# Sums of the merge, the projections and the FFN on VectorE, and each branch for both token halves

## The chip, the core and the metric

The program runs on one core of a Trainium2 chip. A core has a matrix engine (TensorE; the profile calls it PE, and its weight loads PEld), a vector engine (VectorE, DVE), a scalar engine (ScalarE, ACT), a general engine (GpSimd, POOL) and a sync engine (SyncE, SP) which here issues every DMA. Each engine takes its instructions from a queue of its own, in order; semaphores tie the queues together. The metric is the device time of one execution in microseconds. Three runs of the kernel took 1720.38, 1725.53 and 1726.62 us; the median is 1725.53.

## The reference

One layer of a decoder over 1024 tokens of width 1024, all in float32:

```
merged = gate_a * (y_a @ w_branch_a) + gate_b * (y_b @ w_branch_b)
x = x + gate1 * (merged @ w_out)
h2 = rms_norm(x, norm2_gain) * (1 + scale2) + shift2
ffn = (silu(h2 @ ffn_w1) * (h2 @ ffn_w3)) @ ffn_w2
x = x + gate2 * ffn
```

`y_a` (1024x512) is the output of an RWKV-7 recurrence and `y_b` (1024x512) that of sliding-window attention; both, and the gates, come from an input projection of the normed x. `gate1`, `shift2`, `scale2` and `gate2` are sections of a vector made from the conditioning input. The FFN's inner width is 2816.

## The kernel before

Every matmul of float32 operands is done as three (`mm3`, L140 to L144): each operand is split into a rounded part (`hi`, ScalarE) and the rest (`lo`, VectorE), and PE adds lo x hi, hi x lo and hi x hi. A matmul here is mostly 128x128 against 128x512. So each operand needs one ScalarE cast and one VectorE subtraction of a 128x512 tile (or 128x1024, `load_split`, L114) before PE can use it.

The program has five stages. The mixer (0 to about 828 us) runs the recurrence and the attention and leaves `y_a`, `y_b` and the gates in DRAM, transposed: features on partitions, tokens along the row, in two halves of 512 tokens. Then come the branches, the output projection with the second norm, the FFN's first two matrices and the FFN's out projection.

In `branches` (L1001) one token half h is done at a time. For each of eight column blocks j it loads and splits 128 columns of both branch weights (one 128x1024 tile), loads the two gate tiles, and for each branch i runs 4 k x 3 matmuls into a PSUM bank; VectorE multiplies the bank by the gate (L1019), and `sub` (L1054), which is GpSimd's `tensor_tensor` unless another engine is named, adds the two (L1022). That is 192 matmuls for a half. `after0` and `after1` (L1168, L1188) put the loads of the output projection's weights (`wo`, multiplied by `gate1b`, L1166) and its sums beside the branches.

The output projection is a Strassen-like form with seven products of 512x512x512 in place of eight (`token_product`, L1065), 4 jj x 4 t x 3 = 48 matmuls each. Its operands are sums of the quadrants: S1o to S4o from the merged activations, T1o and the `wo_t2` to `wo_t4` from the weights, each a 128x512 `sub`. The order on PE is: branches of half 0, two products (which need half 0 only, into the banks `ya` and `xa`), branches of half 1 (into `xa`, `banks`, L1015), the five other products. `norm2(0)` (L1109) runs beside the last two products: it scales rows, transposes blocks on PE (L1132) and splits them; `norm2(1)` follows and makes also the B operands of the FFN, with two GpSimd subtractions in each of four steps (L1149, L1153).

The FFN works on 11 pairs of column blocks (jp), 7 products x 24 matmuls each (`hidden_first`, `hidden_rest`, L1268, L1278). For each jp there are eight sums of weights (s1, s2, s3, s4 for two i) and four sums of the results (`fs`, L1327 to L1334) on GpSimd; the sums that read PSUM are on VectorE already. The out projection has seven products of 11 jj (132 matmuls each) with weights `w2t` summed on GpSimd, and `finish` (L1379) has two GpSimd instructions for each of 16 less 4 output tiles.

The code of these stages is put in order by a scheduler that knows the dependencies; the place of an instruction in its engine's queue is fixed when the program is built. Names in the profile are those of the tiles: `gt`, `mg`, `wo`, `s1o`, `wpart` (a split weight or operand), `fs`, `s` (an FFN weight sum), `pgf` and `pgo` (PSUM banks), `ptr` (a transpose).

Of the kernel before, what the change touches and what calls it, by code (L numbers as in the profile page):

```python
# [19 lines left out]
P = 128  # L20
# [46 lines left out]
def block_kernel(ctx: ExitStack, tc: tile.TileContext, a: dict, out: bass.AP):  # L67
# [99 lines left out]
    def load_y(h, stage):  # L167
        ys = []
        for src, nm in ((ya_d, "ya"), (yb_d, "yb")):
            for p in range(NP):  # L170
                full = stage()
                nc.sync.dma_start(out=full, in_=src[h, p])
                ys.append(spl(full, f"{nm}{h}_{p}"))
        return ys
# [3 lines left out]
    with ExitStack() as mx:  # L178
# [716 lines left out]
        for h in range(NH):  # L895
# [33 lines left out]
            if h == NH - 1:  # L929
                wkx.close()  # L930
                act2 = ctx.enter_context(tc.tile_pool(name="act2", bufs=NB, side="right"))
                stages = iter(("ada_a", "ada_w") * 4)
                ys0 = load_y(0, lambda: mw.tile([P, HALF], F32, tag=next(stages), name="yst",
                                                bufs=1))
# [6 lines left out]
            for j in range(16):  # L941
                ps = proj_block(hT, 20 + j)
                gt = mw.tile([P, HALF + 1], F32, tag="tm", name="gt", bufs=3)

                nc.scalar.activation(out=gt[:, 0:HALF], in_=ps, func=AF.Tanh, scale=0.5,
                                     bias=hbg[:, j:j + 1])
                nc.sync.dma_start(out=gates_d[h, j], in_=gt[:, 0:HALF])


    with ExitStack() as fx:  # L950
# [50 lines left out]
        def branches(h, ys, banks=None, after=None):  # L1001
            mg = []
            for j in range(KT):
                cols = slice(j * P, (j + 1) * P)
                wh, wl = load_split(
                    lambda v: [(v[:, 0:4, :], wa_d[:, cols].rearrange("(k p) n -> p k n", p=P)),
                               (v[0:64, 4:8, :], wb_v[0, :, :, cols]),
                               (v[64:128, 4:8, :], wb_v[1, :, :, cols])], KT, P)
                gts = []
                for i in range(2):  # L1010
                    gt = st_tile("gt2")
                    nc.sync.dma_start(out=gt, in_=gates_d[h, 8 * i + j])
                    gts.append(gt)
                for i in range(2):
                    ps = banks[(2 * j + i) % 4] if banks else bank()  # L1015
                    for k in range(4 * i, 4 * i + 4):
                        mm3(ps, wh[:, k, :], wl[:, k, :], ys[k][0], ys[k][1], k % 4 == 0,
                            k % 4 == 3)
                    nc.vector.scalar_tensor_tensor(out=gts[i], in0=gts[i], scalar=1.0, in1=ps,  # L1019
                                                   op0=ALU.add, op1=ALU.mult)  # L1020
                mg.append(a_tile("mg"))
                sub(mg[j], gts[0], gts[1], ALU.add)  # L1022
                if after:
                    after(j, mg)
            return mg
# [83 lines left out]
        def norm2(h):  # L1109
# [35 lines left out]
            for k in range(4):  # L1145
# [3 lines left out]
                nc.gpsimd.tensor_tensor(out=t3, in0=b22, in1=b12, op=ALU.subtract)  # L1149
# [3 lines left out]
                nc.gpsimd.tensor_tensor(out=b12, in0=b22, in1=b12, op=ALU.subtract)  # L1153
# [4 lines left out]
        for i in range(3):  # L1158
            ada_loads(i, lambda: a_tile("acc2"))
        WO = {}  # L1160

        def wo_load(e, n, jj):
            WO[e, n, jj] = w = a_tile("wo")
# [4 lines left out]
        def after0(j, mg):  # L1168
            if j == 1:
                ada_section(0, gate1b)  # L1170
            if j in (2, 3, 4, 5):
                wo_load(0, 0, j - 2)
                wo_load(1, 0, j - 2)

        mg0 = branches(0, ys0, None, after0)
        ys1 = load_y(1, lambda: st_tile("yst"))
# [3 lines left out]
        token_product(xa, 4, lambda jj: mg0[2 * jj + 1], lambda jj: WO[1, 0, jj], True)  # L1180
        for t in range(4):
            sub(p1[t], p1[t], x_load(t, 0), ALU.add)
            x1[t][0] = sub(p1[t], xa[t], p1[t], ALU.add, nc.vector)
        ada_section(1, sh2)
        ada_section(2, sc2)
        S1o, S2o, S3o, S4o, T1o = ([None] * 4 for _ in range(5))

        def after1(j, mg):  # L1188
            jj = j // 2
            if j % 2 == 0:  # L1190
                wo_load(0, 1, jj)
                wo_load(1, 1, jj)
                T1o[jj] = sub(a_tile("t1o"), WO[0, 1, jj], WO[0, 0, jj])
                return
            a11, a12, a21, a22 = mg0[j - 1], mg0[j], mg[j - 1], mg[j]
            S1o[jj] = sub(a_tile("s1o"), a21, a22, ALU.add)
            S3o[jj] = sub(a21, a11, a21)
            S2o[jj] = sub(a_tile("s2o"), S1o[jj], a11)
            S4o[jj] = sub(a_tile("s4o"), a12, S2o[jj])
# [5 lines left out]
        def wo_t2(jj):  # L1205
            return sub(T1o[jj], WO[1, 1, jj], T1o[jj])

        def wo_t3(jj):
            return sub(WO[0, 1, jj], WO[1, 1, jj], WO[0, 1, jj])

        def wo_t4(jj):
            return sub(WO[1, 0, jj], WO[1, 0, jj], T1o[jj])

        token_product(ya, 4, lambda jj: S2o[jj], wo_t2, False)
        u1 = copies(ya, "u1")
        token_product(xa, 4, lambda jj: S4o[jj], lambda jj: WO[1, 1, jj], False)
        for t in range(4):
            sub(u1[t], u1[t], x_load(t, 1), ALU.add)
            x1[t][1] = sub(u1[t], xa[t], u1[t], ALU.add, nc.vector)
        norm2(0)  # L1220
        token_product(ya, 4, lambda jj: S3o[jj], wo_t3, False)
        for t in range(4):
            sub(p5[t], p5[t], x_load(4 + t, 1), ALU.add)
            x1[4 + t][1] = sub(p5[t], ya[t], p5[t], ALU.add, nc.vector)
            x1[4 + t][0] = x_load(4 + t, 0, temp)
        token_product(ya, 4, lambda jj: mg1[2 * jj + 1], wo_t4, False)
        for t in range(4):
            sub(x1[4 + t][0], ya[t], x1[4 + t][0], ALU.add, nc.vector)
# [49 lines left out]
        def hidden_rest(jp, ws, u2, f11):  # L1278
# [19 lines left out]
            for i in range(2):  # L1298
                sub(u2[i], ps[i], u2[i], ALU.add, nc.vector)
# [3 lines left out]
            for i in range(2):  # L1303
                u3[i] = temp("u3")
                sub(u3[i], ps[i], u2[i], ALU.add, nc.vector)
            ps = dense(lambda i: ws[i][3], "T4")
            for i in range(2):
                c[i] = temp("c21")
                sub(c[i], u3[i], ps[i], ALU.subtract, nc.vector)
# [4 lines left out]
            for i in range(2):  # L1314
                sub(u3[i], ps[i], u3[i], ALU.add, nc.vector)
# [3 lines left out]
            for i in range(2):  # L1319
                sub(u2[i], ps[i], u2[i], ALU.add, nc.vector)  # L1320
# [136 lines left out]
```

## Time and profile before

| | |
|---|---|
| runs, median | 1725.53 us (1720.38 to 1726.62) |
| profiled execution, its own time | 1723.27 us |
| span of the profiled execution, first to last instruction | 1720.8 us |
| PE busy | 1592.9 us, 93% |
| DVE, ACT, POOL busy | 67%, 41%, 34% of the span |
| mean granted TensorE clock | 0.963 of full speed |

The profiled execution is the one from which every row below is taken; 2.5 us of its time lie outside the span. PE's busy time counts matmuls in flight, so a stretch in which PE is busy from end to end can still be one in which it is slow: the granted clock tells that. The engines' shares are means over five stages with different limits.

### The profile page before, as it was taken

Reading aid. Unit: us, or ns where it says so; the run is one execution under the profiler, and the core shown is the slowest. Engines: PE = TensorE matmul, PEld = TensorE weight load, DVE = VectorE, ACT = ScalarE, POOL = GpSimd, SP = SyncE. Lnnn points to the kernel's source line nnn. Section 1 sums busy time; section 2 is a strip of 40 time slices with the busy share of each in tenths; the row PEclk is TensorE's granted clock in tenths of the full one; section 3 lists DMA queues with packets and bytes.
Section 4 is the critical chain, followed back from the end, with each engine's and each line's share of the span. In section 5 each row is a group of like instructions: output and inputs, shape, how many; then the busy total and the mean of one; then the engine's idle time right before and its main releaser. Section 6 shows DMA issues by size and latency. Waiting matters only on the chain. (4 is left out here: it accounts for less than half of the span.)

```text
span 1720.8 us, 24983 instructions
## 1 busy us (share of the span) xinstructions
PE 1592.9 (93%) x8835; PEld 1218.1 (71%) x8835; DVE 1156.2 (67%) x2560; ACT 712.1 (41%) x1346; POOL 579.1 (34%) x504
## 2 busy tenths in 40 slices
PE   3989988999989999999988698899999999999998
PEld 2756766666656777667877576687777777786887
DVE  7689777775567767875364577765555555689566
ACT  5454435445643233446241257323323332343442
POOL 6232121122331000000247821563333334689022
PEclk9998999999997998999999798999999999999999
DMA  9344446345443224325765235343323322871641
GB/s 306 101 138 128 118 130 169 111 127 176 124 128 93 58 79 108 96 77 181 223 184 160 68 120 156 122 153 120 101 92 98 97 94 74 287 253 60 198 151 50
DMA packets 234081, 228.19 MB, mean 133 GB/s; under 512 B 38850, under 2 KB 171084, under 8 KB 233956
## 3 DMA queue, kind: packets, MB, share of 16 engines
q1 hardware_dynamic: 233956, 226.60, 43.2%
q8 instruction: 69, 1.13, 0.3%
q14 instruction: 56, 0.46, 0.1%
HBM read 175.92 MB, written 50.63 MB: 132 GB/s over the span
## 5 line engine op out<-in xcount | busy, mean ns | idle before, releaser
L142 PE MATMUL pg<-hhi,wlo 128*128 128x512 f32 x480 | 201.9, 423 | 8.6 <-DVE wlo L134 5.5
L143 PE MATMUL pg<-hlo,whi 128*128 128x512 f32 x480 | 202.1, 421 | 0.0
L144 PE MATMUL pg<-hhi,whi 128*128 128x512 f32 x480 | 201.3, 420 | 0.0
L142 PE MATMUL pgo<-wpart 128*128 128x512 f32 x420 | 167.8, 399 | 15.0 <-DVE wpart L1051 7.8
L134 DVE TENSOR_TENSOR wlo<-wraw,whi 128x1024 fp32r<-128x1024 f32 x88 | 111.8, 1274 | 94.5 <-ACT whi L133 90.1
L143 PE MATMUL pgo<-wpart 128*128 128x512 f32 x420 | 167.8, 399 | 4.2 <-DVE wpart L1051 4.2
L144 PE MATMUL pgo<-wpart 128*128 128x512 f32 x420 | 166.7, 397 | 0.0
L885 POOL TENSOR_TENSOR aacc<-aacc,adaw 128x512 f32<-128x512 f32 x64 | 86.6, 1353 | 234.9 <-ACT adaw L884 221.6
L1051 DVE TENSOR_TENSOR wpart<-s,wpart 128x512 fp32r<-128x512 f32 x88 | 84.5, 960 | 85.8 <-ACT wpart L1050 83.8
L133 ACT CAST whi<-wraw 128x1024 fp32r<-128x1024 f32 x88 | 91.6, 1047 | 113.5 <-PE pg L144 56.3
L1055 POOL TENSOR_TENSOR fs<-fs 128x512 f32<-128x512 f32 x44 | 59.5, 1364 | 188.2 <-DVE fs L1260 186.6
L142 PEld LDWEIGHTS pg<-hhi,wlo 128*128 128x128 f32 x480 | 94.0, 196 | 35.9 <-DVE wlo L134 5.7
L1051 DVE TENSOR_TENSOR wpart<-fo,wpart 128x512 fp32r<-128x512 f32 x77 | 86.2, 1120 | 46.6 <-ACT wpart L1050 46.6
L1050 ACT CAST wpart<-s 128x512 fp32r<-128x512 f32 x88 | 54.6, 622 | 150.5 <-PE pgf L144 91.2
L143 PEld LDWEIGHTS pg<-hlo,whi 128*128 128x128 f32 x480 | 93.8, 195 | 21.6 <-issue 3.0
L144 PEld LDWEIGHTS pg<-hhi,whi 128*128 128x128 f32 x480 | 94.0, 196 | 20.0 <-issue 1.1
L142 PEld LDWEIGHTS pgo<-wpart 128*128 128x128 f32 x420 | 80.8, 192 | 34.4 <-DVE wpart L1051 9.1
L1055 DVE TENSOR_TENSOR u<-pgf,u 128x512 f32<-128x512 f32 x88 | 60.5, 687 | 60.8 <-PE pgf L144 60.7
L1050 ACT CAST wpart<-fo 128x512 fp32r<-128x512 f32 x77 | 47.9, 622 | 122.6 <-PE pgo L144 106.3
L143 PEld LDWEIGHTS pgo<-wpart 128*128 128x128 f32 x420 | 80.7, 192 | 24.0 <-DVE wpart L1051 7.6
L144 PEld LDWEIGHTS pgo<-wpart 128*128 128x128 f32 x420 | 80.7, 192 | 16.6
L619 DVE SCALAR_TENSOR_TENSOR tmpi<-ai,inv,rt 128x60 f32<-128x60 f32 (+24 forms) x248 | 71.8, 290 | 16.8 <-DMA ai<-a_scr 12.7
(583 smaller groups left out, 4126.8 us busy)
## 6 DMA issues: line engine op xcount, KB each, us to landing
wraw<-in_w_in_dram SPq DMA_DIRECT2D x72, 512.0 KB
wraw<-in_ffn_w_dram SPq DMA_DIRECT2D x56, 512.0 KB
f_d<-fs SPq DMA_DIRECT2D x77, 256.0 KB
fo<-f_d SPq DMA_DIRECT2D x77, 256.0 KB
adaw<-in_ada_w_dram SPq DMA_DIRECT2D x64, 256.0 KB
w2t<-in_ffn_w_dram SPq DMA_DIRECT2D x44, 256.0 KB
adaw<-in_ada_w_dram SPq DMA_DIRECT2D x8, 1024.0 KB
gates_d<-gt SPq DMA_DIRECT2D x32, 256.0 KB
```

The costliest lines, as they stand in the source:

```text
L133: nc.scalar.copy(out=hi, in_=raw)
L134: nc.vector.tensor_tensor(out=lo, in0=raw, in1=hi.bitcast(F32), op=ALU.subtract)
L142: nc.tensor.matmul(ps, lhsT=ll, rhs=rh, start=first, stop=False, skip_group_check=more)
L143: nc.tensor.matmul(ps, lhsT=lh, rhs=rl, start=False, stop=False, skip_group_check=more)
L144: nc.tensor.matmul(ps, lhsT=lh, rhs=rh, start=False, stop=last, skip_group_check=more)
L619: nc.vector.scalar_tensor_tensor(out=tv, in0=ai[:, jj, j + 1:32].unsqueeze(1).broadcast_to([P, m, n]), scalar=inv2[:, j:j + 1], in1=rt[:, ...
L885: nc.gpsimd.tensor_tensor(out=acc, in0=acc, in1=wt, op=ALU.add)
L1050: nc.scalar.copy(out=hi, in_=src)
L1051: nc.vector.tensor_tensor(out=lo, in0=src, in1=hi.bitcast(F32), op=ALU.subtract)
L1055: (eng or nc.gpsimd).tensor_tensor(out=out, in0=x, in1=y, op=op)
```

## The change

1. `sub` runs on VectorE, and with it every elementwise sum and product from the merge on, those of `norm2` and `finish` too. GpSimd has no work after the mixer; its queue shrinks from 391 rows to 180.
2. `branches(h)` becomes `branch(i)`: branch 1 (attention) for both token halves, then branch 0 for both. A weight tile is loaded and split once in a branch, 128x512, and used by both halves. Branch 1's gate tile is loaded into the `mg` tile and multiplied in place; branch 0's result is added to it.
3. The `wo` tiles and T1o to T4o are made in branch 1 (`after_b`), S1o to S4o in branch 0 (`after_a`). Three `y` parts are loaded and split in the mixer's last part, where there were two; `ysa[1]` is loaded between the branches.
4. The seven products stand in a row behind the branches. The third to the fifth are now S2, S1, S4 (before: S1, S2, S4).

```diff
-        def branches(h, ys, banks=None, after=None):
-            mg = []
+        def branch(i, ys, after):
+
             for j in range(KT):
                 cols = slice(j * P, (j + 1) * P)
                 wh, wl = load_split(
-                    lambda v: [(v[:, 0:4, :], wa_d[:, cols].rearrange("(k p) n -> p k n", p=P)),
-                               (v[0:64, 4:8, :], wb_v[0, :, :, cols]),
-                               (v[64:128, 4:8, :], wb_v[1, :, :, cols])], KT, P)
...
+                    lambda v: [(v[0:64], wb_v[0, :, :, cols]), (v[64:128], wb_v[1, :, :, cols])]
+                    if i else [(v, wa_d[:, cols].rearrange("(k p) n -> p k n", p=P))], 4, P)
+                for h in range(NH):
+                    gt = a_tile("mg") if i else st_tile("gt2")
                     nc.sync.dma_start(out=gt, in_=gates_d[h, 8 * i + j])
...
+                    ps = bank()
+                    for k in range(4):
+                        mm3(ps, wh[:, k, :], wl[:, k, :], ys[h][k][0], ys[h][k][1], k == 0, k == 3)
+                    nc.vector.scalar_tensor_tensor(out=gt, in0=gt, scalar=1.0, in1=ps,
                                                    op0=ALU.add, op1=ALU.mult)
-                mg.append(a_tile("mg"))
-                sub(mg[j], gts[0], gts[1], ALU.add)
...
+                    if i:
+                        mg[h].append(gt)
+                    else:
+                        sub(mg[h][j], mg[h][j], gt, ALU.add)
+                after(j)
...
-        def sub(out, x, y, op=ALU.subtract, eng=None):
-            (eng or nc.gpsimd).tensor_tensor(out=out, in0=x, in1=y, op=op)
+        def sub(out, x, y, op=ALU.subtract):
+            nc.vector.tensor_tensor(out=out, in0=x, in1=y, op=op)
             return out
...
+        def after_b(j):
+            if j == 0:
+                ada_section(0, gate1b)
+            if 1 <= j < 5:
+                for jj in range(4):
+                    wo_load(*((0, 0), (1, 0), (0, 1), (1, 1))[j - 1], jj)
+            if 4 <= j:
+                jj = j - 4
+                b11, b21, b12, b22 = (WO[x + (jj,)] for x in ((0, 0), (1, 0), (0, 1), (1, 1)))
+                T3o[jj] = sub(a_tile("t3o"), b22, b12)
+                T1o[jj] = sub(b12, b12, b11)
+                T2o[jj] = sub(a_tile("t2o"), b22, b12)
+                T4o[jj] = sub(a_tile("t4o"), b21, T2o[jj])
...
+        def after_a(j):
             if j == 1:
...
+                ada_section(1, sh2)
+                ada_section(2, sc2)
+            if j % 2 == 0:
+                return
+            jj = j // 2
+            a11, a12, a21, a22 = mg[0][j - 1], mg[0][j], mg[1][j - 1], mg[1][j]
+            S1o[jj] = sub(a_tile("s1o"), a21, a22, ALU.add)
+            S2o[jj] = sub(a_tile("s2o"), S1o[jj], a11)
+            S4o[jj] = sub(a_tile("s4o"), a12, S2o[jj])
+            S3o[jj] = sub(a21, a11, a21)
+
+        mg = [[], []]
+        ysa = [ysa0, None]
+        branch(1, ysb, after_b)
+        ysa[1] = load_y(ya_d, 1, lambda: st_tile("yst"))
+        branch(0, ysa, after_a)
         xa, ya = four(1), four(0)
-        token_product(ya, 4, lambda jj: mg0[2 * jj], lambda jj: WO[0, 0, jj], True)
+        token_product(ya, 4, lambda jj: mg[0][2 * jj], lambda jj: WO[0, 0, jj], True)
         p1 = copies(ya, "p1")
...
-        mg1 = branches(1, ys1, xa, after1)
+        token_product(ya, 4, lambda jj: S2o[jj], lambda jj: T2o[jj], False)
+        u1 = copies(ya, "u1")
         token_product(xa, 4, lambda jj: S1o[jj], lambda jj: T1o[jj], True)
         p5 = copies(xa, "p5")
...
         token_product(xa, 4, lambda jj: S4o[jj], lambda jj: WO[1, 1, jj], False)
```

On PE the 192 matmuls of the first branch are now followed at once by those of the second, and the first output product stands behind 384 branch matmuls.

On DVE, at the end of one FFN step and the start of the next, before: `u` and `fs` are results of the step that ends, `s` the weight sums of the next, `wraw` loaded weights.

```order
L1055 TENSOR_TENSOR u_12428<-pgf,u_12428 128x512
L1051 TENSOR_TENSOR wpart<-wraw,wpart 128x512
L1260 TENSOR_TENSOR fs<-fs,u_12428 128x512
L1051 TENSOR_TENSOR wpart<-s_12736,wpart 128x512
L1051 TENSOR_TENSOR wpart<-s_12740,wpart 128x512
L1051 TENSOR_TENSOR wpart<-s_12776,wpart 128x512
L1260 TENSOR_TENSOR fs<-fs,pgf 128x512
L1051 TENSOR_TENSOR wpart<-s_12779,wpart 128x512
```

The sums that make `s`, and the four `fs` sums of L1327 to L1334, are not in this queue: GpSimd makes them. (`fs<-fs,u` is the product of L1260.)

The same place of a step after the change:

```order
L1054 TENSOR_TENSOR u_13842<-pgf,u_13842 128x512
L1050 TENSOR_TENSOR wpart<-wraw,wpart 128x512
L1258 TENSOR_TENSOR fs<-fs,u_13842 128x512
L1054 TENSOR_TENSOR fs<-fs 128x512 x4
L1054 TENSOR_TENSOR s_14149<-wraw 128x512
L1054 TENSOR_TENSOR s_14150<-s_14149,wraw 128x512
L1054 TENSOR_TENSOR s_14153<-wraw 128x512
L1054 TENSOR_TENSOR s_14154<-s_14153,wraw 128x512
L1050 TENSOR_TENSOR wpart<-s_14150,wpart 128x512
L1054 TENSOR_TENSOR s_14190<-wraw 128x512
L1050 TENSOR_TENSOR wpart<-s_14154,wpart 128x512
L1054 TENSOR_TENSOR s_14193<-wraw 128x512
```

The four result sums (one row, `x4`) and the first four weight sums now stand between the last result and the first split of the next step; the other four follow between the splits.

On SP, at the end of branch 1 and the start of branch 0, after the change: `wraw` are branch weights, `mg` and `gt` gate tiles, `yst` the blocks of `ysa[1]`.

```order
L127 DMA wraw<-in_w_branch_a_dram 128x4x128
L1166 DMA wo<-in_w_out_dram 128x512 x2
L1014 DMA mg<-gates_d 128x512
L1166 DMA wo<-in_w_out_dram 128x512 x3
L127 DMA wraw<-in_w_branch_a_dram 128x4x128
L1166 DMA wo<-in_w_out_dram 128x512
L1014 DMA mg<-gates_d 128x512 x2
L1166 DMA wo<-in_w_out_dram 128x512 x2
L127 DMA wraw<-in_w_branch_a_dram 128x4x128
L1166 DMA wo<-in_w_out_dram 128x512 x2
L171 DMA yst<-ya_d 128x512 x4
L1014 DMA gt_9808<-gates_d 128x512
```

Gate loads, `wo` loads, the weights of the next branch and the `y` blocks share the one queue, and a weight load stands there until a `wraw` buffer is free.

The queue in the second half's branches before:

```order
L1012 DMA gt_10073<-gates_d 128x512
L1012 DMA gt_10075<-gates_d 128x512
L1012 DMA gt_10121<-gates_d 128x512
L127 DMA wraw<-in_w_branch_a_dram 128x4x128
L127 DMA wraw<-in_w_branch_b_dram 64x4x128
L127 DMA wraw<-in_w_branch_a_dram 128x4x128
L127 DMA wraw<-in_w_branch_b_dram 64x4x128
L127 DMA wraw<-in_w_branch_a_dram 128x4x128 x2
L127 DMA wraw<-in_w_branch_b_dram 64x4x128 x6
```

Each column block had three weight loads (both branches) and two gate loads there, for one half; now a column block of a branch has one weight load (two in branch 1) for both halves.

## Rows read from the trace of the kernel before

**Rows 1.** The windows by stage: busy time (and count) of each engine, clock, DMA.

```profile
...
core 0: us, PE busy (x) PEld busy (x) DVE busy (x) ACT busy (x) POOL busy (x), PEclk, DMA share, GB/s
...
870.00:945.00 75.00, 66.74 (x283) 53.46 (x282) 41.81 (x49) 22.28 (x35) 42.40 (x28) 0.98 0.63 178
945.00:985.00 40.00, 24.76 (x73) 18.52 (x74) 19.38 (x18) 11.07 (x21) 38.19 (x28) 0.74 0.22 72
985.00:1050.00 65.00, 58.36 (x270) 47.18 (x270) 50.56 (x118) 36.24 (x77) 11.03 (x8) 0.92 0.45 143
1050.00:1110.00 60.00, 50.20 (x204) 38.12 (x203) 41.28 (x52) 31.63 (x54) 28.69 (x19) 0.91 0.43 131
...
1160.00:1480.00 320.00, 313.43 (x1361) 253.81 (x1360) 170.31 (x226) 98.94 (x164) 136.61 (x98) 1.00 0.32 105
1480.00:1600.00 120.00, 113.41 (x490) 90.91 (x489) 108.54 (x95) 50.10 (x91) 90.98 (x56) 1.00 0.59 200
...
```

**Rows 2.** PE's timeline: first branch matmul, first FFN matmul, end; start us first.

```profile
...
827.76 0.50 PE L142 MATMUL pgf<-ya_0h,wlo 128*128 128x512 f32 x1
...
1037.53 0.40 PE L142 MATMUL pgf<-g0h,wpart 128*128 128x512 f32 x1
...
1713.25 0.39 PE L142 MATMUL pgo<-wpart 128*128 128x512 f32 x1
...
1715.74 0.39 PE L144 MATMUL pgo<-wpart 128*128 128x512 f32 x1
```

**Rows 3.** What PE waits for, 870 to 1110 us: us in total, times, longest.

```profile
PE pgo L142 <- DVE gt L1019: 11.4, 3, 5.5
PE pgo L142 <- DVE wpart L1051: 7.8, 2, 5.2
PE pgf L142 <- ACT bt_3h L1101: 5.1, 1, 5.1
PE ptr L1132 <- DVE xr L1126: 3.8, 1, 3.8
PE pgf L142 <- ACT u L1274: 3.7, 2, 3.3
...
```

**Rows 4.** DVE's instructions by line and form, 1110 to 1720 us.

```profile
...
L1051 DVE TENSOR_TENSOR wpart<-fo,wpart 128x512 fp32r<-128x512 f32 x77 | 86.2, 1120 | 46.6 <-ACT wpart L1050 46.6
...
L1055 DVE TENSOR_TENSOR u<-pgf,u 128x512 f32<-128x512 f32 x85 | 58.4, 687 | 56.7 <-PE pgf L144 56.7
...
L1051 DVE TENSOR_TENSOR wpart<-t1o,wpart 128x512 fp32r<-128x512 f32 x11 | 7.5, 684 | 0.0
...
```

**Rows 5.** What SP's queue waits for, 827 to 1045 us.

```profile
...
SPq L1012 <- POOL mg L1055: 34.0, 7, 7.5
...
```

**Rows 6.** The timeline of all engines at one FFN step's end, start us first.

```profile
...
1338.99 0.69 DVE L1055 TENSOR_TENSOR u<-pgf,u 128x512 f32<-128x512 f32 x1 [1.33 <-PE pgf L144]
...
1341.06 5.26 POOL L1055 TENSOR_TENSOR fs<-fs 128x512 f32<-128x512 f32 x4 [22.38 <-DVE fs L1260]
...
1348.97 0.62 ACT L1050 CAST wpart<-s 128x512 fp32r<-128x512 f32 x1 [3.84 <-POOL s L1055]
...
1349.62 1.11 DVE L1051 TENSOR_TENSOR wpart<-s,wpart 128x512 fp32r<-128x512 f32 x1 [8.64 <-ACT wpart L1050]
...
1350.79 0.50 PE L142 MATMUL pgf<-bt_0h,wpart 128*128 128x512 f32 x1 [0.82 <-DVE wpart L1051]
...
```

**Rows 7.** What PE waits for, 1160 to 1480 us.

```profile
PE pgf L142 <- DVE wpart L1051: 6.6, 8, 0.8
```

**Rows 8.** What PE waits for, 1480 to 1720 us.

```profile
PE pgo L143 <- DVE wpart L1051: 4.2, 8, 1.7
PE pgf L142 <- DVE u L1055: 2.4, 1, 2.4
```

**Rows 9.** The windows view of 20 us of the out projection.

```profile
1540.00:1560.00 20.00, 20.00 (x90) 16.58 (x89) 20.00 (x13) 8.12 (x15) 20.00 (x12) 1.00 0.32 95
```

**Rows 10.** What POOL waits for, 1480 to 1720 us.

```profile
...
POOL w2t L1055 <- DMA w2t<-in_ffn_w_dram: 11.2, 2, 10.4
...
```

More of the change, by code (lines that the diff above doesn't have):

```diff
@@ L165, in spl, with load_y @@
         return hi, lo
-    def load_y(h, stage):
+    def load_y(src, h, stage):
         ys = []
[L169 to L173, printed above, removed]
+        for p in range(NP):
+            full = stage()
+            nc.sync.dma_start(out=full, in_=src[h, p])
+            ys.append(spl(full, f"y{h}_{p}"))
         return ys
@@ L931, in block_kernel, with stage @@
                 act2 = ctx.enter_context(tc.tile_pool(name="act2", bufs=NB, side="right"))
-                stages = iter(("ada_a", "ada_w") * 4)
-                ys0 = load_y(0, lambda: mw.tile([P, HALF], F32, tag=next(stages), name="yst",
-                                                bufs=1))
+                stages = iter(("ada_a", "ada_w") * 6)
+                def stage():
+                    return mw.tile([P, HALF], F32, tag=next(stages), name="yst", bufs=1)
+                ysb = [load_y(yb_d, 0, stage)]
+                ysa0 = load_y(ya_d, 0, stage)
             mixer_step(h, NP, hT)
@@ L947, in block_kernel @@
                 nc.sync.dma_start(out=gates_d[h, j], in_=gt[:, 0:HALF])
+        ysb.append(load_y(yb_d, 1, stage))
     with ExitStack() as fx:
@@ L1158, in block_kernel @@
         for i in range(3):
-            ada_loads(i, lambda: a_tile("acc2"))
+            ada_loads(i, lambda: xp.tile([P, HALF], F32, tag="h4", name="acc2", bufs=4))
         WO = {}
+        T1o, T2o, T3o, T4o = ([None] * 4 for _ in range(4))
         def wo_load(e, n, jj):
-            WO[e, n, jj] = w = a_tile("wo")
+            WO[e, n, jj] = w = temp("wo")
             r0 = (2 * jj + e) * P
@@ new lines, in block_kernel @@
+        S1o, S2o, S3o, S4o = ([None] * 4 for _ in range(4))
+        def after_a(j):
+            if j == 1:
+                ada_section(1, sh2)
[8 more added lines that the diff above has]
+            S3o[jj] = sub(a21, a11, a21)
@@ L1181, in block_kernel @@
         for t in range(4):
             sub(p1[t], p1[t], x_load(t, 0), ALU.add)
[L1183 to L1199, printed above, removed]
@@ L1218, in block_kernel @@
             sub(u1[t], u1[t], x_load(t, 1), ALU.add)
[L1219 removed]
+            x1[t][1] = sub(u1[t], xa[t], u1[t], ALU.add)
         norm2(0)
[L1221 removed]
+        token_product(ya, 4, lambda jj: S3o[jj], lambda jj: T3o[jj], False)
         for t in range(4):
             sub(p5[t], p5[t], x_load(4 + t, 1), ALU.add)
[L1224 removed]
+            x1[4 + t][1] = sub(p5[t], ya[t], p5[t], ALU.add)
             x1[4 + t][0] = x_load(4 + t, 0, temp)
[L1226 removed]
+        token_product(ya, 4, lambda jj: mg[1][2 * jj + 1], lambda jj: T4o[jj], False)
         for t in range(4):
[L1228 removed]
+            sub(x1[4 + t][0], ya[t], x1[4 + t][0], ALU.add)
         norm2(1)
@@ L1308, in hidden_rest @@
                 c[i] = temp("c21")
-                sub(c[i], u3[i], ps[i], ALU.subtract, nc.vector)
+                sub(c[i], u3[i], ps[i])
                 s4[i] = s2[i]
```

54 lines of the change are left out of this document (13 added, 41 removed).

## The prediction

> **What bounds the kernel now.** I read the windows by stage first. PE is the engine on which everything ends: in the middle of the FFN it is busy 313.4 of 320 us at a granted clock of 1.00, so its matmuls set the time there. The loss lies between 870 and 1110 us: PE is idle 8.3 us of 75, 15.2 of 40, 6.6 of 65 and 9.8 of 60, and in the same windows its granted clock is 0.98, 0.74, 0.92 and 0.91 [rows 1]. POOL is busy 38.2 of 40 us in the worst of them, 945 to 985.
>
> The timeline gives the size of it. At full clock twelve matmuls start from 1713.25 to 1715.74, 2.49/11 = 0.2264 us each. From the first branch matmul (827.76) to the first FFN matmul (1037.53) are 209.8 us [rows 2]. In it stand 384 matmuls of the branches and 336 of the seven products, 720 x 0.2264 = 163.0 us. So 46.8 us are something else. By the windows, PE's idle time to 1050 is 30.1 us, less the 3.8 us wait for `xr` [rows 3], which lies behind 1037.53: 26.3. The lower clock takes 0.02 x 75 + 0.26 x 40 + 0.08 x 65 = 17.1 us [rows 1]. That is 43.4 of the 46.8; the remaining 3.4 are norm2's transposes and other small matmuls, which stay.
>
> Then the waits of PE. The longest entries are `pgo` on DVE's gate product `gt` (11.4 us in 3 waits) and on `wpart` (7.8 in 2) [rows 3]. The first is a bank or a gate tile that comes late; SP shows why: its gate loads waited 34.0 us, in 7 waits, for POOL's `mg` sums, which free the tiles [rows 5]. The order of work adds to it: half 1's branches can only come behind two products whose operands are sums on POOL.
>
> **The change, part by part.** *What a moved sum costs.* A VectorE instruction of this shape takes 684 ns where POOL is quiet (`t1o`) and 687 ns with a PSUM operand, but 1120 ns for `fo`, read while POOL works [rows 4]. In 1540 to 1560 both engines are busy 20.0 of 20 us with 13 and 12 instructions: 1.5 and 1.7 us each [rows 9]. At 0.69 us the 25 would take 17.2 us on one engine. So I take 0.69 us for each moved sum and 0.69 for those that stay. The other end is that VectorE's slow instructions are slow for another reason and stay so: 108.54/95 = 1.14 us [rows 1]. I take the low end because 684 and 687 ns were seen in the same stretch as 1120.
>
> The Trainium skill (SBUF — State Buffer, "Who interferes with whom") says that a VectorE instruction with two SBUF inputs contends with a GpSimd instruction that reads SBUF, one blocking until the other is done, and that one with at most one SBUF input does not. By that rule a moved sum costs VectorE no more than the blocking it took away, as the 25 instructions in 20 us say. The rule also speaks against the change in one point: the results read from PSUM ran beside POOL freely, and now share a queue with its sums.
>
> *Branches and output projection.* PE's work is the same 720 matmuls; the order is now 384 branch matmuls, then seven products. Waits that go: SP no longer waits for POOL's `mg`, and the split of a branch weight is 128x512. VectorE must keep up. A column block takes PE 24 x 0.2264 = 5.43 us. In branch 1 VectorE has for it one split, two gate products and, averaged over eight blocks, four weight sums and scalings: 7 x 0.69 = 4.8 us. In branch 0 it has one split, two gate products, two `mg` sums and two S sums, again 4.8 us, and beside these four splits of `ysa[1]` (2.8 us) and some 12 early splits of the first products (8.3 us): 8 x 4.8 + 11.1 = 49.5 us for PE's 43.4. The 6 us too many are hidden by the six PSUM banks (2.7 us of PE's work each) and by the products, where VectorE has two splits per 12 matmuls (1.4 of 2.7 us).
>
> What comes late next: `ysa[1]`. Its four loads stand in SP's queue behind weight loads that wait for a `wraw` buffer, and its splits stand in VectorE's queue behind the last gate product of branch 1. PE wants it 2.7 us after branch 0 starts. The bounds are 0 and 7.5 us, the longest SP wait for `mg` [rows 5]; I take 4, the middle. I keep 1 us for the copies of the fourth product's bank, which the fifth (into the same banks) waits for, 3 for norm2(0)'s transposes, whose chain is as it was, and 5 for the lower clock after such waits (17.1 us of it came with 26.3 of waits; 8 of waits bring 5 in that proportion). That leaves 13 of 43.4 lost: **30 us gained**; bounds from the same terms 20 and 40.
>
> *norm2(1) and the FFN's start.* Between 1037 and 1110 PE loses 3.8 + 9.8 us idle and 0.09 x 60 = 5.4 to the clock, 19 in all. Two of its four waits (`xr`, ACT's `u`) have no POOL in front [rows 3]; behind `bt_3h` (5.1 us) stand two POOL subtractions per step. At most 19 and, since VectorE has 41.3 of 60 us there and now gets 19 instructions more (13 us), perhaps a loss of 5. I take **5 us gained**.
>
> *FFN.* The step's end shows the wait that goes. VectorE has the last `u` at 1338.99; POOL's four `fs` sums end at 1346.32 (1341.06 + 5.26), its weight sums follow, and ACT can cast at 1348.97; VectorE's split takes 1.11 us and PE stands 0.82 [rows 6]. After the change VectorE does from 1338.99 on three instructions, four `fs` and four weight sums, 11 x 0.69 = 7.6 us: 1346.6; the cast of the second sum lies beside, and the split ends at 1347.3. PE wants it at 1350.79 - 0.82 = 1349.97, so 2.7 us are left and the wait is gone. There are 8 such waits, 6.6 us [rows 7], and with the refill of PE behind each (0.50 us instead of 0.39 for the first matmul, some 0.2 in all) **8 us gained**. VectorE's own load: (226 + 98) x 0.69 = 224 us of 320 [rows 1].
>
> *Out projection.* PE is idle 6.6 us between 1480 and 1600: 2.4 for a `u` and 4.2 in eight waits for `wpart` [rows 8]. VectorE's 95 and POOL's 56 instructions there are 151 x 0.69 = 104 us of 120. What is late next is a `w2t` sum: POOL waited 10.4 us at once for a load [rows 10], and that wait would now stand in VectorE's queue. So between 0 and 6.6, less up to 10; I take **5 gained**.
>
> *Sum.* 30 + 5 + 8 + 5 = 48 us. The profiled execution took 1723.27 us (span 1720.8 and 2.5 around it): 1675.3. The median of the runs is 2.26 above that execution: 1677.5, and I write 1677.
>
> **The rivals.** *A, VectorE's one queue makes the branches wait.* Sums that wait for a load (`wo`, gate, x) stand ahead of a gate product that would free a bank; PE waits as before, only for fewer microseconds. For it: 49.5 us of work in 43.4 in branch 0. Against: six banks. Half of the 30 is lost: 1692. *B, nearly all goes.* `ysa[1]` comes in time, so no wait brings a lower clock; 9 of the 13 lost are back, and the FFN's start gives 14 instead of 5: 48 + 18 = 66, 1659. For it: the granted clock was 1.00 in the FFN, where no wait of PE is over 0.8 us [rows 1, 7]. *C, slower: VectorE's price does not fall.* At 1.14 us the 151 instructions of 1480 to 1600 take 172 us, 52 more than the window; less the 30 and the 8 and the 5 elsewhere that is 9 us slower, 1735. It decides from 120/151 = 0.79 us per instruction on. Against: 684 ns with POOL quiet [rows 4]. *D, no gain.* The waits of 870 to 1050 are not POOL's doing but follow from weights and gates that SP loads late; the new order makes other waits of equal size: about 1725. For it: the gate loads of the kernel after still stand in one queue with weight loads that wait for a buffer. Against: 34.0 us of SP's waiting was for POOL alone [rows 5], and the branch weights' splits are halved.
>
> The Trainium skill (Perfetto Trace Analysis, "Optimizing Scalar/DVE Operations") warns that, since the two engines share a read port, moving operations between them might not help. That would be D's result as far as the sums go. The trace agrees that both together gain little over one: 25 instructions took 20.0 us [rows 9].
>
> **How the numbers follow.** Chances: the forecast 0.54, A 0.20, B 0.17, D 0.04, C 0.05. The forecast's own range, from its terms (30 by 10 either way, 5 by 5 and more, 5 by 5), is 1664 to 1691. Taking in A and most of B, but not C and D, the range is 1656 to 1701. Faster by over 0.5% (8.6 us, about what a measurement here can tell from no change) come the forecast, A and B: 0.91. Within 0.5% D: 0.04. Slower C: 0.05.
>
> **What would show it.** In the profile after: POOL has nothing behind the mixer. From the first branch matmul to the first FFN matmul about 180 us instead of 209.8 (30 less), the windows of it at a clock of 0.95 or more. `wpart` splits at 0.69 us in every form; no PE wait at an FFN step's end; VectorE busy some 0.7 of the FFN. If the first stretch is above 195 us with PE waiting for a gate product, it is A; if `wpart` or `s` stay above 0.8 us, it is C. The forecast would be wrong outright if VectorE stood waiting for DMAs of `w2t` or `wraw` with finished banks behind it.

## The result and the profile after

The changed kernel took 1657.75 us (median of 4 runs, 1651.00 to 1662.81) against 1722.95 for the kernel before (4 runs, one more than above, 1715.36 to 1726.62): a ratio of 0.9625, 95% interval 0.9575 to 0.9674. Measured again beside another set of runs it took 1661.78 against 1721.66, a ratio of 0.9663 (0.9622 to 0.9703). It is faster, inside the range of 1656 to 1701, but 19 us below the forecast of 1677 and nearest to rival B (1659).

Its windows by stage come first; the columns are those of [rows 1].

```profile
...
core 0: us, PE busy (x) PEld busy (x) DVE busy (x) ACT busy (x) POOL busy (x), PEclk, DMA share, GB/s
...
870.00:945.00 75.00, 69.81 (x296) 57.33 (x297) 61.01 (x100) 21.91 (x39) 0.00 (x0) 0.93 0.31 98
945.00:985.00 40.00, 39.85 (x178) 32.66 (x178) 27.75 (x68) 24.10 (x50) 0.00 (x0) 1.00 0.26 85
985.00:1050.00 65.00, 58.90 (x266) 45.53 (x265) 54.39 (x113) 44.91 (x84) 0.00 (x0) 0.95 0.61 191
1050.00:1110.00 60.00, 60.00 (x266) 49.46 (x265) 51.60 (x84) 19.78 (x32) 0.00 (x0) 1.00 0.47 151
...
1160.00:1480.00 320.00, 319.81 (x1411) 264.59 (x1410) 237.01 (x366) 113.76 (x188) 0.00 (x0) 1.00 0.44 146
...
```

POOL's column is empty. In the middle of the FFN PE is idle 0.2 us of 320 instead of 6.6, and 1411 matmuls are recorded there instead of 1361. Between 945 and 985 the clock is 1.00 where it was 0.74. VectorE is busier than before: 237 of 320 us in the FFN (170 before), 61 of 75 between 870 and 945 (42 before). The kernel after is 13 us ahead at the first branch matmul and 39 us at the first FFN matmul, so the same microseconds hold later work.

The timeline of PE gives the ends of the stretches, as in [rows 2]: the first branch matmul, the first FFN matmul, the last matmul.

```profile
...
814.87 0.50 PE L142 MATMUL pgf<-y_0h,wlo 128*128 128x512 f32 x1 [1.29 <-ACT gt L948]
...
998.97 0.39 PE L142 MATMUL pgf<-g0h,wpart 128*128 128x512 f32 x1
...
1643.95 0.39 PE L144 MATMUL pgo<-wpart 128*128 128x512 f32 x1
...
```

From the first branch matmul to the first FFN matmul are 184.1 us (209.8 before), from there to the end 645.0 (678.2 before). The mixer ended 12.9 us earlier in this pair of profiles, which was not forecast.

PE's waits from the branches to the FFN's start, which answer to [rows 3]:

```profile
...
PE pgf L143 <- DVE y_0l L164: 5.2, 1, 5.2
PE ptr L1131 <- DVE xr L1125: 4.3, 1, 4.3
PE pgf L142 <- ACT u L1272: 1.5, 1, 1.5
PE psg L975 <- issue: 1.0, 1, 1.0
...
```

The waits for `gt`, `wpart` and `bt_3h` (24.3 us) are gone; the wait for `xr` is as it was, and one for `y_0l`, a block of `ysa[1]`, is new. VectorE's instructions behind the first FFN matmuls, by line and form as in [rows 4]:

```profile
...
L1054 DVE TENSOR_TENSOR u<-pgf,u 128x512 f32<-128x512 f32 x88 | 60.7, 691 | 67.9 <-PE pgf L144 66.8
L1050 DVE TENSOR_TENSOR wpart<-s,wpart 128x512 fp32r<-128x512 f32 x88 | 60.5, 690 | 0.3
L1050 DVE TENSOR_TENSOR wpart<-fo,wpart 128x512 fp32r<-128x512 f32 x77 | 53.1, 690 | 54.3 <-ACT wpart L1049 54.2
...
L1054 DVE TENSOR_TENSOR s<-wraw 128x512 f32<-128x512 f32 x44 | 29.9, 686 | 0.0
L1054 DVE TENSOR_TENSOR fs<-fs 128x512 f32<-128x512 f32 x44 | 29.4, 689 | 0.9
...
```

Every form takes 0.69 us now, `wpart<-fo` 690 ns for 1120. The timeline at the end of one FFN step, as in [rows 6]; the last row is PE's:

```profile
...
1358.29 0.69 DVE L1054 TENSOR_TENSOR u<-pgf,u 128x512 f32<-128x512 f32 x1 [1.33 <-PE pgf L144]
...
1360.32 2.75 DVE L1054 TENSOR_TENSOR fs<-fs 128x512 f32<-128x512 f32 x4
...
1363.69 0.69 DVE L1054 TENSOR_TENSOR s<-s,wraw 128x512 f32<-128x512 f32 x1
...
1365.63 0.69 DVE L1050 TENSOR_TENSOR wpart<-s,wpart 128x512 fp32r<-128x512 f32 x1
...
1368.97 0.39 PE L142 MATMUL pgf<-bt_0h,wpart 128*128 128x512 f32 x1
...
```

The four `fs` sums take 2.75 us (POOL took 5.26), the second weight sum ends at 1364.38, its split at 1366.32, and PE uses it at 1368.97 without a gap: 2.65 us to spare, for 2.7 worked out ahead.

A steady FFN step as a whole runs from one first `g0h` matmul to that of the next step. Before:

```profile
...
1220.09 0.40 PE L142 MATMUL pgf<-g0h,wpart 128*128 128x512 f32 x1
...
1259.66 0.40 PE L142 MATMUL pgf<-g0h,wpart 128*128 128x512 f32 x1
...
```

And after:

```profile
...
1167.69 0.39 PE L142 MATMUL pgf<-g0h,wpart 128*128 128x512 f32 x1
...
1205.77 0.39 PE L142 MATMUL pgf<-g0h,wpart 128*128 128x512 f32 x1
...
```

39.57 us became 38.08; 168 matmuls at 0.2264 are 38.04. A step lost 1.5 us before, and only 0.82 of it shows as idle time of PE [rows 6].

### The profile page after: what moved, and what is told of

It reads as the page before. It is cut to its first block, busy times and chain, and to the rows that moved or that the text cites. A ratio compares the mean times of both kernels' runs of the same rounds, so it can differ in the third digit from the quotient of the medians.

```text
span 1649.2 us, 24811 instructions
## 1 busy us (share of the span) xinstructions
PE 1557.9 (94%) x8835; PEld 1202.4 (73%) x8835; DVE 1199.2 (73%) x2844; ACT 709.2 (43%) x1346; POOL 157.9 (10%) x220
## 4 chain that ended last, share of the span: by engine, by line
PE 63%; DMA 5%; DVE 4%; ACT 2%; issue 1%; SPq 1%; POOL 0%; DVEq 0%; ACTq 0%
PE pgf L143 9%; PE pgf L142 9%; PE pgf L144 9%; PE pgo L144 5%; PE pgo L143 5%; PE pgo L142 5%; PE pg L144 3%; PE pg L142 3%; PE pg L143 3%; DMA ai<-a_scr 1%; DMA mg<-gates_d 1%; DMA wo<-in_w_out_dram 1%; DMA adaw<-in_ada_w_dram 1%; PE pgq L142 1%; PE pgq L143 1%; PE pgq L144 1%
## 5 line engine op out<-in xcount | busy, mean ns | idle before, releaser
L143 PE MATMUL pgo<-wpart 128*128 128x512 f32 x420 | 163.8, 390 | 0.2 <-DVE wpart L1050 0.2
L144 PE MATMUL pgo<-wpart 128*128 128x512 f32 x420 | 163.9, 390 | 0.0
L142 PE MATMUL pgo<-wpart 128*128 128x512 f32 x420 | 163.4, 390 | 0.0
L134 DVE TENSOR_TENSOR wlo<-wraw,whi 128x1024 fp32r<-128x1024 f32 (+1 forms) x88 | 100.8, 1148 | 59.1 <-ACT whi L133 58.8
L133 ACT CAST whi<-wraw 128x1024 fp32r<-128x1024 f32 (+1 forms) x88 | 85.1, 969 | 131.6 <-PE pgf L144 59.2
L143 PEld LDWEIGHTS pg<-hlo,whi 128*128 128x128 f32 x480 | 92.6, 193 | 21.1 <-issue 2.7
L144 PEld LDWEIGHTS pg<-hhi,whi 128*128 128x128 f32 x480 | 92.6, 193 | 19.7 <-issue 1.1
L1050 DVE TENSOR_TENSOR wpart<-fo,wpart 128x512 fp32r<-128x512 f32 x77 | 53.1, 690 | 54.3 <-ACT wpart L1049 54.2
L618 DVE SCALAR_TENSOR_TENSOR tmpi<-ai,inv,rt 128x60 f32<-128x60 f32 (+24 forms) x248 | 75.2, 303 | 22.8 <-DMA ai<-a_scr 18.8
L143 PEld LDWEIGHTS pgo<-wpart 128*128 128x128 f32 x420 | 78.8, 188 | 16.9 <-DVE wpart L1050 0.6
L142 PEld LDWEIGHTS pgo<-wpart 128*128 128x128 f32 x420 | 78.8, 188 | 16.4 <-DVE wpart L1050 0.3
L144 PEld LDWEIGHTS pgo<-wpart 128*128 128x128 f32 x420 | 78.9, 188 | 16.1
L1049 ACT CAST wpart<-wraw 128x512 fp32r<-128x512 f32 x66 | 40.9, 622 | 102.5 <-PE pgf L144 101.4
L883 ACT ACTIVATE adaw<-adaw,vT 128x512 f32<-128x512 f32 x64 | 46.2, 722 | 76.4 <-DMA adaw<-in_ada_w_dram 76.0
```

The lines of the kernel that those rows point to most:

```text
L133: nc.scalar.copy(out=hi, in_=raw)
L134: nc.vector.tensor_tensor(out=lo, in0=raw, in1=hi.bitcast(F32), op=ALU.subtract)
L142: nc.tensor.matmul(ps, lhsT=ll, rhs=rh, start=first, stop=False, skip_group_check=more)
L143: nc.tensor.matmul(ps, lhsT=lh, rhs=rl, start=False, stop=False, skip_group_check=more)
L144: nc.tensor.matmul(ps, lhsT=lh, rhs=rh, start=False, stop=last, skip_group_check=more)
L618: nc.vector.scalar_tensor_tensor(out=tv, in0=ai[:, jj, j + 1:32].unsqueeze(1).broadcast_to([P, m, n]), scalar=inv2[:, j:j + 1], in1=rt[:, ...
```

## The experiments

The table holds each profile's stretches in us, worked from the starts of the same matmuls: a, where the first branch matmul lies (the mixer's length); b, from there to the first FFN matmul; c, from there to the end of PE's work; and, inside c, d, from the first `bt_0h` matmul to the first out-projection matmul. In a full-clock row without gaps b would hold 163.0 us of matmuls and d 1704 x 0.2264 = 385.8.

| kernel | a | b | c | d |
|---|---|---|---|---|
| before, twice | 827.8, 828.0 | 209.8, 210.6 | 678.2, 677.5 | 409.5, 409.1 |
| after, twice | 814.9, 821.8 | 184.1, 183.7 | 645.0, 643.3 | 386.4, 386.4 |
| x1, old order, VectorE, twice | 830.2, 832.1 | 179.4, 179.9 | 645.4, 645.5 | 387.8, 387.8 |
| x2, new order, GpSimd | 823.1 | 199.2 | 679.7 | 410.6 |
| y1, `ysa[1]` early | 825.2 | 181.8 | 643.2 | 386.4 |
| y2, gates first | 827.2 | 184.1 | 643.9 | 386.4 |
| y3, both | 826.9 | 175.3 | 645.1 | 386.4 |
| c1, GpSimd reads | 823.5 | 184.1 | 707.0 | 444.1 |
| c2, GpSimd writes | 825.1 | 185.8 | 646.2 | 387.1 |
| c3, more on VectorE | 828.2 | 183.5 | 674.8 | 413.0 |
| c4, s3 and s4 on GpSimd | 816.9 | 183.6 | 647.3 | 388.7 |

Two profiles of one kernel agree within 2 us in b, c and d, so these tell causes apart, also where a kernel has one profile; a does not repeat.

**The two parts apart.** x1 is the kernel before with this edit alone (and the same for `t3`, `T2` and `finish`):

```diff
-            (eng or nc.gpsimd).tensor_tensor(out=out, in0=x, in1=y, op=op)
+            nc.vector.tensor_tensor(out=out, in0=x, in1=y, op=op)
```

> The kernel before, with its order of branches and products, and every elementwise sum from the merge on moved to VectorE. Theory (the sums' price is a term of its own): from the first FFN matmul to the last matmul 645 us as in the kernel after (678 before), from the first branch matmul to the first FFN matmul 195 us (209.8 before, 184.1 after), so some 1675 us in all. Rival 1 (the FFN's gain comes from the new order, for example from freer buffers): 678 and 209.8, no gain. Rival 2 (the sums do it all, the order nothing): 645 and 184, 1660 us.

It took 1655.25 us (1651.99 to 1662.33), ratio 0.9623 (0.9583 to 0.9662). The first branch matmul and the first FFN matmul in its profile:

```profile
...
830.20 0.50 PE L142 MATMUL pgf<-ya_0h,wlo 128*128 128x512 f32 x1
...
1009.58 0.40 PE L142 MATMUL pgf<-g0h,wpart 128*128 128x512 f32 x1
...
```

That is rival 2: the sums do it all. Its gate loads still wait on SP for `mg` sums, now VectorE's, from 827 to 1012 us:

```profile
...
SPq L1012 <- DVE mg L1055: 23.0, 10, 4.3
...
```

But PE has no wait for a gate product left in the branches, and its longest wait there is 1.8 us. A second measurement was made beside the last kernels below:

> The kernel before with all sums on VectorE, once more, beside the others of this call. Theory: the old order with the sums on VectorE is as good as the new one or a few microseconds better (179.4 us against 184 from the first branch matmul to the first FFN matmul), so 1653 to 1662 us. Rival: the 1655 us of the first time were chance, and it is 5 us or more slower than the kernel after (1658 to 1662).

1659.75 us (1654.34 to 1664.82), ratio 0.962 (0.958 to 0.966), b 179.9: not chance.

x2 is the kernel after with every sum that the kernel before had on GpSimd put back there; its core is

```diff
-            nc.vector.tensor_tensor(out=out, in0=x, in1=y, op=op)
+            (eng or nc.gpsimd).tensor_tensor(out=out, in0=x, in1=y, op=op)
```

> The kernel after, with its order, and the sums that the kernel before had on GpSimd put back there. Theory: 678 us from the first FFN matmul to the end, and in the branches and products GpSimd has some 64 sums of 1.5 us in 87 us, which come late: 195 us or more, 1710 us in all. Rival 1 (the order does the FFN's gain): 645 us there. Rival 2 (the sums do it all): 210 us and 678 us, no gain over the kernel before.

1703.89 us (1698.69 to 1708.72), ratio 0.9888 (0.9846 to 0.9931). As its theory said, the FFN is as slow as before; the branches gain 10.6 us. Its window of the branches shows POOL busier than VectorE, 92.6 against 58.4 us of 127:

```profile
...
823.00:950.00 127.00, 112.50 (x479) 90.63 (x480) 58.42 (x70) 24.15 (x43) 92.60 (x67) 0.93 0.50 157
...
```

So the new order is worth 11 us in b while GpSimd makes the sums, and costs 4 to 5 once VectorE makes them (184.1 and 183.7 against 179.4 and 179.9).

**The spread.**

> The kernel after once more, to see the spread. Its mixer has the same instructions in the same order on PE as that of the kernel before, up to the first branch matmul, but ended 12.9 us earlier in the profile (814.9 against 827.8). Theory (the mixer's length changes from run to run): the first branch matmul lies anywhere between 812 and 830 us in these four profiles, without regard to the kernel, while the stretches behind it repeat within 2 us. Rival (the change shortens the mixer): 815 in both kernels with the new order, 828 in those with the old.

> The kernel before once more, for the spread of its stretches: 209.8 and 678.2 us within 2 us each. Theory: the first branch matmul anywhere between 812 and 830 us. Rival: 828.

b, c and d repeat. The mixer's end lay at 821.8 and 828.0. Over all fourteen profiles a runs from 814.9 to 832.1, from 814.9 to 828.2 in the ten with the new order and from 827.8 to 832.1 in the four with the old. The first instructions that differ are SP's loads of y in the mixer's second half (524 us in the profile after). Before that the same instructions ran at another granted clock. The first 300 us of x1's second profile:

```profile
...
0.00:300.00 300.00, 247.44 (x1644) 183.70 (x1645) 224.83 (x640) 138.69 (x253) 85.11 (x132) 0.91 0.51 147
...
```

And those of the kernel after:

```profile
...
0.00:300.00 300.00, 247.48 (x1752) 183.20 (x1754) 233.64 (x683) 145.97 (x267) 87.57 (x134) 0.95 0.54 157
...
```

0.91 there and 0.95 here, in the first 300 us, is nothing that the change can have made. SP's first load of y lies anywhere between 524.1 and 539.3 us, so 15 of the 17 us of spread arise before the kernels differ. From that load to the first branch matmul are 290.9 to 297.5 us in the four profiles with the old order (mean 293.1) and 289.2 to 293.1 in the ten with the new (mean 291.1): the new order's own part in a is about 2 us, if it is more than spread.

**Price of contention.** c1 adds to the kernel after, in each FFN step,

```diff
+            for i in range(2):
+                for _ in range(6):
+                    nc.gpsimd.tensor_tensor(out=view(jk), in0=s1[i], in1=view(gate2b[:, 0:HALF]),
+                                            op=ALU.add)
```

> The kernel after, with 12 GpSimd sums in each FFN step that read two SBUF tiles and whose result nobody uses; the output is unchanged. Theory 1 (GpSimd's reading slows VectorE's instructions with two SBUF inputs): while they run, VectorE's splits and weight sums go from 0.69 us to 1.0 or more, and the sums that read PSUM stay at 0.69. Theory 2 (what cost time before was the wait for GpSimd's results, not the slower VectorE): from the first FFN matmul to the last matmul still within 5 us of 645, since nobody waits for these sums. Rival to 2 (the slower VectorE was the cost): 660 us or more, PE waiting for wpart in most steps.

1721.28 us (one run): the FFN's stretch d is 58 us longer, though its profile has no wait for POOL from the first FFN matmul on. VectorE's instructions by line and form, 1060 to 1480 us:

```profile
...
L1050 DVE TENSOR_TENSOR wpart<-s,wpart 128x512 fp32r<-128x512 f32 x84 | 95.8, 1143 | 0.2
L1054 DVE TENSOR_TENSOR s<-wraw 128x512 f32<-128x512 f32 x42 | 63.4, 1516 | 0.0
L1054 DVE TENSOR_TENSOR u<-pgf,u 128x512 f32<-128x512 f32 x81 | 55.4, 684 | 33.8 <-PE pgf L144 33.7
...
```

What PE waits for, 1100 to 1440 us:

```profile
...
PE pgf L142 <- DVE wpart L1050: 19.4, 32, 1.3
...
```

The splits take 1143 ns and the weight sums 1516, the results read from PSUM still 684. PE waits for splits 32 times. Theory 1 holds and theory 2 falls: in this kernel the slower VectorE is enough to lose the gain of the FFN and more. c2 replaces eleven of the twelve sums by `memset`:

```diff
+            for _ in range(24):
+                nc.gpsimd.memset(jk, 0.0)
```

> The kernel after, with one such GpSimd sum and 24 GpSimd memsets of a 128x512 tile in each FFN step, results unused. Theory 1: a GpSimd instruction that only writes leaves VectorE's instructions at 0.69 us. Rival (any GpSimd work slows VectorE): 1.0 us or more as with the reading sums.

1663.84 us (one run). POOL's writes, by line, in the same stretch:

```profile
...
L1300 POOL MEMSET jk<- 128x512 f32 x262 | 138.2, 527 | 15.1
...
```

And VectorE's instructions beside them:

```profile
...
L1050 DVE TENSOR_TENSOR wpart<-s,wpart 128x512 fp32r<-128x512 f32 x88 | 68.9, 785 | 0.2
...
L1054 DVE TENSOR_TENSOR s<-wraw 128x512 f32<-128x512 f32 x42 | 28.4, 681 | 0.0
...
```

138 us of writing on GpSimd leave the weight sums at 681 ns and d at 387.1; the 785 ns of the splits hold the eight that ran beside the one reading sum of a step (1.79 us each; the others 0.67 to 0.69). The Trainium skill (SBUF — State Buffer, "Who interferes with whom") says that two SBUF inputs on VectorE contend with a GpSimd instruction that reads SBUF, not with one that only writes, and that a VectorE instruction with at most one SBUF input does not contend. The traces agree in all three: 1143 ns (c1), 681 ns (c2), and 684 ns with a PSUM operand (c1).

c4 puts only s3 and s4 back on GpSimd (the edit for s4 is the same):

```diff
-                sub(s3[i], ws[i][0], ws[i][1])
+                sub(s3[i], ws[i][0], ws[i][1], ALU.subtract, nc.gpsimd)
```

> The kernel after, with four of the eight weight sums of an FFN step (s3 and s4, which are needed only for the third and the last product) back on GpSimd. Theory (in the kernel before, a wait came where the chain to the first split ran through GpSimd's sums; away from that chain they cost nothing): from the first FFN matmul to the last matmul within 3 us of 645, although VectorE's instructions beside them take over 0.69 us. Rival (any reading GpSimd sum costs PE time through the slower VectorE): 650 us or more.

1654.57 us (one run), c 647.3, as the theory said, and d 388.7, 2.4 over the kernel after. VectorE's splits:

```profile
...
L1050 DVE TENSOR_TENSOR wpart<-s,wpart 128x512 fp32r<-128x512 f32 x84 | 67.8, 816 | 2.1
...
```

The mean rises from 690 to 816 ns and PE hardly feels it. Four sums away from the chain cost little, twelve cost 58 us; how the 23 us of the kernel before divide between waiting for GpSimd's results and slower splits, these runs do not say. [Rows 6] give an estimate for one steady step: with a split of 0.69 in place of 1.11 us PE's wait of 0.82 would have been some 0.4 us, so about half of it was the slower split and half POOL's late sum. For the branches and the FFN's start nothing here divides the two.

**VectorE's room.** c3 has c1's twelve sums on VectorE (`nc.vector` for `nc.gpsimd`).

> The kernel after, with 12 more VectorE sums in each FFN step, results unused: 8.3 us more on VectorE per step of 38 us, which has 26 before. Theory (VectorE has room left in the FFN): from the first FFN matmul to the last matmul at most 5 us longer than 645. Rival (the one VectorE queue is near its bound, as in the recorded rival C): a third of the 11 x 8.3 = 91 us or more is seen, 675 us.

1693.94 us (one run), c 674.8, the rival's number; d is 413.0, some 27 us longer. But the loss does not lie in the steady steps:

```profile
...
1064.00:1160.00 96.00, 81.32 (x320) 65.58 (x321) 77.59 (x127) 21.85 (x36) 0.00 (x0) 0.90 0.32 104
1160.00:1440.00 280.00, 278.92 (x1223) 228.65 (x1223) 235.34 (x374) 88.95 (x146) 0.00 (x0) 1.00 0.29 98
...
```

In the steady steps (168 matmuls, 38 us) VectorE is busy 235 of 280 us and PE idle 1.1. The loss lies in the first 96 us: 14.7 idle and a clock of 0.90. The first three steps have no `hidden_first` beside them, 120 matmuls or 27 us, for the same sums on VectorE. So VectorE has room left in the steady steps, as the theory said, and the rival is right for the first ones.

**The wait for `ysa[1]`.** y1 loads it with the others:

```diff
         ysb.append(load_y(yb_d, 1, stage))
+        ysa1 = load_y(ya_d, 1, stage)
```

> The kernel after, with the second half's RWKV blocks (ysa[1]) loaded and split in the mixer's last part, as the three others are, not between the branches. Theory: the 5.2 us wait of PE for y_0l and the lower clock behind it (0.91 to 0.93 over 75 us, some 5 to 7 us) go: from the first branch matmul to the first FFN matmul 174 us (184 before this edit); the time 8 to 10 us below that of the kernel after. Rival 1 (VectorE is what makes it late): the wait moves to another place, 184 us. Rival 2: the four splits more at the mixer's end delay the first branch matmul by as much as is won.

1660.35 us (1657.39 to 1665.60), b 181.8: 2 us of the 10 forecast. Rival 1: the wait moved. The longest of PE's waits in the branches:

```profile
...
PE pgf L142 <- DVE mg L1019: 4.3, 1, 4.3
...
```

SP's queue at the place, in its timeline:

```profile
...
870.27 0.38 SPq L127 DMA_DIRECT2D wraw<-in_w_branch_a_dram  x1
870.69 0.98 SPq L1167 DMA_DIRECT2D wo<-in_w_out_dram  x2
871.71 1.85 SPq L1015 DMA_DIRECT2D gt<-gates_d  x4
876.92 0.38 SPq L127 DMA_DIRECT2D wraw<-in_w_branch_a_dram  x1
877.35 0.98 SPq L1015 DMA_DIRECT2D mg<-gates_d  x2
...
```

The last two `mg` gate loads were issued at 877.35, behind a weight load at 876.92 that had to wait for a buffer. y2 issues all gate loads of branch 1 ahead of the branch and leaves `ysa[1]` where it was:

```diff
+        for j in range(KT):
+            for h in range(NH):
+                mgt[h].append(a_tile("mg"))
+                nc.sync.dma_start(out=mgt[h][j], in_=gates_d[h, 8 + j])
         branch(1, ysb, after_b)
```

> The kernel after, with all 16 gate loads of branch 1 issued ahead of the branch's code, so that in SP's queue they stand ahead of the w_out loads and of most weight loads. Theory (in branch 1 gate loads stand in SP's queue behind weight loads that wait for a buffer, so the gate products, the sums and the splits of ysa[1] behind them in VectorE's queue come late): the 5.2 us wait for y_0l falls under 2 us, from the first branch matmul to the first FFN matmul 176 us (184 before this edit). Rival (VectorE is full there, or ysa[1]'s own loads are late): 182 to 184 us.

1663.71 us (1658.71 to 1665.30), b 184.1, the wait for `y_0l` 5.7: no gain by itself, the rival. y3 has both edits.

> The kernel after with both edits, ysa[1] in the mixer and the gate loads of branch 1 first. Theory: neither the wait for y_0l nor the 4.3 us wait for a gate product that took its place when ysa[1] alone was early; 174 us from the first branch matmul to the first FFN matmul, the time some 8 us below the kernel after. Rival (VectorE or the weights' loads are the limit in the branches): 180 us or more.

1654.64 us (1646.02 to 1660.05), ratio 0.959 (0.9551 to 0.963), b 175.3, where 174 was forecast. Its windows, b as a whole and the change of branches:

```profile
...
826.85:1002.15 175.30, 173.39 (x788) 142.14 (x789) 131.89 (x241) 64.52 (x120) 0.00 (x0) 1.00 0.50 162
870.00:945.00 75.00, 74.49 (x329) 61.35 (x328) 71.80 (x120) 21.92 (x39) 0.00 (x0) 1.00 0.42 133
...
```

PE is idle 0.5 of 75 us at the change of branches (5.2 in the kernel after) at a clock of 1.00 (0.93), with VectorE busy 71.8. Each of the two late loads hid the other; both had to go. By the stretches y3 is the best of the kernels tried, 820.4 us behind the mixer against 824.8 and 825.4 for x1 and 827.0 to 829.1 for the kernel after; the medians, with the mixer's spread on them, part it from x1 and the kernel after by 0.6 to 7 us, less than the runs of one kernel differ.

## Why the prediction was right, and where not

*Price of a moved sum:* right. 0.69 us was taken, 0.69 measured in every form. c1 shows that the other end, 1.14 us, is what contention costs (1143 ns), and that at this price the gain is gone (d 444.1).

*Branches and output projection:* 30 us forecast, 25.7 and 26.9 measured in b. Of the terms that were to remain, 4 us for `ysa[1]` were 5.2 and 3 for norm2(0) nearly nothing, and VectorE carried the load. Around the wait for `ysa[1]` the clock was 0.93, under the 0.95 that was to be a sign. What could go at all was put too high: in y3 (one profile) PE is idle 1.9 us of this stretch at a clock of 1.00, and it still takes 175.3 us, 12.3 above the 163.0 where 3.4 had been left. So some 34.5 of the 209.8 us could go, not 43.4. The windows' lower clock was counted for PE's idle time too, and of the 5.2 us taken for it from 985 to 1050, 3.4 lie behind 1037.53 (a clock of 0.73 from there to 1050). That "the order of work adds to it" held only beside GpSimd's sums: the new order alone gains 10.6 us (x2), but x1 gains 30.4 without it. Nor did SP's waiting measure the loss: 34.0 us for `mg` [rows 5] were still 23.0 in x1, and PE no longer felt them. The new order's own late loads cost more than its smaller splits gave; without them (y3) it is 4 us below x1.

*FFN's start and FFN:* from the first FFN matmul to the first out-projection matmul 5 + 8 us were forecast, and 2.4 of the out projection's 5 lay there too, 15.4 in all; 462.3 (1499.84 - 1037.53) became 435.3 (1434.25 - 998.97), 27.0. These are the mis-sized terms. The larger error lies in the start: to the end of the first step, 120 matmuls behind the first `bt_0h` (1126.12 before, 1075.21 after), 88.6 us became 76.2, so 12.4 gained for 5. I kept 14 of the 19 lost us there for want of a cause, though the longest wait, `bt_3h`, had two POOL sums per step in front; it vanished. Behind it 373.7 became 359.0, 14.7 for 8 and the 2.4. For the steady stretch I took PE's idle time, 6.6 us in 8 waits [rows 7], and 0.2 for each refill. A matmul's record lasts 0.39 us at a pitch of 0.2264, so idle time starts late and leaves out the refill: a step lost 1.5 us, eight of them 12. The count of matmuls from 1160 to 1480 says nearly the same: 1411 - 1361 = 50 x 0.2264 = 11.3 us.

*Out projection:* 2.6 of the 5 us stood for its `wpart` waits; 215.9 became 209.7, 6.2 gained. VectorE waited 6.1 us for `w2t` loads from 1380 to 1650, and PE did not notice.

*The rest:* 12.9 us of the pair of profiles lie in the mixer and do not repeat; behind the mixer 888.0 became 829.1, 58.9 us for the 48 forecast (61.2 in the second pair). The mechanism was right: with the sums on VectorE each costs 0.69 us and the waits of PE go (x1). That the time lies in the range is in part luck: the forecast's own range, 1664 to 1691, missed it, the branches gave 3 to 4 us less and the FFN with its start 11.6 more than forecast, and 4 to 6 of the 65.2 us between the medians are, by these profiles, not behind the mixer at all. Rival A's sign, a first stretch above 195 us with PE waiting for a gate product, did not come; the wait for `ysa[1]` was a term of the forecast. B came nearest in time, and one of its two reasons held: the FFN's start gave 12.4 of its 14, but `ysa[1]` did not come in time. C fell with the 0.69 us, D with x1.

## What to carry to other kernels

Where two engines are both busy all the time, count their instructions in one window and price them all at the uncontended time: if that fits, one engine alone may be faster, as here, and unused work on the second can cost as much as the first had gained. Measure what a matmul stream loses by the matmuls missing from a window, times the pitch, and not by the idle time that a wait view shows. And run the parts of a change apart: here the change of engine made all of the gain, and the reordering beside it cost 4 to 5 us until two loads in its queue were moved together.

## What was not expected of the hardware

Twelve GpSimd sums per step that nobody used cost 58 us (c1, one run), about 0.4 us for each of the 132. The same instructions at the start of the mixer were granted a clock of 0.91 in one run and 0.95 in another, and the mixers of fourteen profiles ended within 17 us of one another. One wait of 5.2 us between the branches went with a clock of 0.93 from 870 to 945 us, and in y3, without the wait, it was 1.00 there.
